# 48 float32r test matmuls behind the last product of a two-block decoder kernel

## The chip, the cores and the metric

The kernel runs on one core of a Trainium2 chip. The metric is device time in microseconds (us); the time before is the median of three runs. TensorE is called PE here, its weight loads PEld, VectorE DVE, ScalarE ACT, GpSimd POOL, and SyncE SP.

## The reference

Two transformer blocks on 256 tokens of width 1024. The part that matters here is the end of the second block, the last thing computed:

```python
h2 = rms_norm(x, norm_ffn_pre[l])
up = causal_depthwise_conv(h2 @ w_up[l], conv_w[l], conv_b[l])
g, v = jnp.split(up, 2, axis=-1)
ff = (jax.nn.gelu(g, approximate=True) * v) @ w_down[l]
x = x + rms_norm(ff, norm_ffn_post[l])
```

The rows of x are the result. All that stands before (two attention forms, a gated recurrence, cross attentions, pooling, a first feed-forward) is untouched by the change.

## The kernel before, in words

Every float32 product with a weight is carried by three float32r products: both operands are split into hi and lo, and hi*hi + hi*lo + lo*hi is accumulated in PSUM (`mm3`, lines 204 to 207). Each of these is one matmul of 128 stationary columns and 256 or 512 moving columns, with its own weight load.

The work is listed as a program of units and short pieces (`place`, `run`, `do`) and emitted in that order by `emit` (line 180). PE's instructions stand in just this order; the other engines take theirs as they are released. The last entries of the program come from `ffn` (line 558), called for the second block's feed-forward: eleven granules of 256 features, of which the last two are held back (`hold=2`). `close(t)` (line 594) issues their down products for token half t, column half by column half, through `down` (line 569) and `mm3`. These write the PSUM tiles named `s`; the moving operand is a weight row of 512 contiguous float32r values. `second` (line 505) closes token half 1, and its last product, L207, is the last instruction of PE before the end of the program.

Behind it stands the end of the computation, in `Last` (line 482) and the helpers that it inherits: ACT squares the column half and sums it (L303), DVE adds the two sums (L309), POOL raises the result to the power -1/2 (L296), DVE multiplies the row by the gain (L434) and adds it to the residual in three column quarters (L474), ACT and POOL do the fourth one (L492, L493), and SP stores each quarter with a DMA (L494). Then the program ends (L1397): every engine waits until its own work is done (DRAIN), SP waits for the stores, and a barrier joins the engines.

PSUM has three groups of tiles: `mm` and `tp` with two buffers each, `s` with four. The `tp` tiles (`tp_t`, line 85) hold transposes and small products; the last use of one in the program is a transpose of the gate columns early in this feed-forward. `xh` and `xl` are the hi and lo parts of the normed, transposed input of the feed-forward, 128 partitions by 8 by 256 values each; `eh` is such a tile for the memory rows.

Of the kernel before, what the change touches and what calls it, by code (L numbers as in the profile page):

```python
# [18 lines left out]
P = 128  # L19
T = 256  # L20
# [10 lines left out]
class Granule:  # L31
    """2048 weights per partition: one load, split in two parts as they are needed."""
# [7 lines left out]
def two_blocks(ctx: ExitStack, tc: tile.TileContext, a: dict, out: bass.AP):  # L40
    """Every float32 product with a weight is carried by three float32r passes:
    both operands are split exactly as hi + lo with hi = float32r(v), lo = v - hi,
    and hi*hi + hi*lo + lo*hi is accumulated in PSUM.

    Stationary/moving forms:
      a_units: weight blocks stationary, x^T moving  -> [feature, token]
      b_units: x^T blocks stationary, weights moving -> [token, feature]

    The work is first listed as a program of units (one weight part each, with short
    pieces attached), then emitted in that order; loads and splits run ahead of it.  # L50
    """
# [19 lines left out]
    # ------------------------------------------------------------------ tiles  # L71
# [38 lines left out]
    # ------------------------------------------------------------------ program and weight stream  # L110
    stream = []
# [53 lines left out]
    def place(fn, gran=None, pieces=()):  # L165
        """Append one unit; gran: the granule that it is the first to use."""
        if gran is not None:
            stream.append(gran)
        prog.append((fn, list(pieces)))

    def run(units, at=None):
        """List the units in order; at[i] are short pieces that follow unit i."""
        at = at or {}
        for i, (fn, gran) in enumerate(units):
            place(fn, gran, at.get(i, ()))
# [4 lines left out]
    def emit():  # L180
        """Per unit: its products, what earlier units left to do, the next split, its own results, its pieces."""
        for fn, pieces in prog:
            evac = fn() if fn is not None else None
            todo = later[:]
            later.clear()
            for f in todo:
                f()
            if fn is not None:
                pump()
            if evac is not None:  # L190
                evac()
            for f in pieces:
                f()

    def then(*fns):
        """Emit the first function in the next unit, the second one in the unit after that, and so on."""
        def go():
            fns[0]()
            if fns[1:]:
                then(*fns[1:])  # L200
        later.append(go)

    # ------------------------------------------------------------------ products
# [5 lines left out]
    def a_units(src, xt, evac, nk=8):  # L209
        """One granule [nk*128, c] (nk*c = 2048) in two units: evac(i, psum[128, 512]) per pair of blocks."""  # L210
# [25 lines left out]
    def b_part(w, xt, t, k0, o, first, last):  # L236
        """o[128 tokens of half t, 512] += x[:, k0*128...] @ w, w = (hi, lo) [128, 2, 512]."""
        tok = slice(t * P, (t + 1) * P)
        for k in range(2):
            mm3(o, r32(xt[0][:, k0 + k, tok]), r32(xt[1][:, k0 + k, tok]), w[0][:, k, :], w[1][:, k, :],  # L240
                first and k == 0, last and k == 1)

    def b_units(src, xt, evac):
        """[token, 512] = x @ w[:, 512 columns] in four units of two k blocks; evac(t, psum[128, 512])."""
# [29 lines left out]
    def grid(w, c0, n, dst, scale=None, xt=XT):  # L274
        """n granules of feature-major output written to dst[128, n*512]."""
        u = []
        for g in range(n):
            u += a_units(cols(w, c0, g), xt, ev_to(dst[:, g * 512:(g + 1) * 512], scale))
        return u

    def rows(w, c0, n, dst, xt=XT):
        """n times 512 columns of token-major output written to dst[128, 2, n*512]."""
# [6 lines left out]
    # ------------------------------------------------------------------ norms  # L289
# [3 lines left out]
    def power(v, n):  # L293
        """v ** -0.5 on [128, n]."""
# [4 lines left out]
    def square(src, acc, eng=S):  # L299
        """acc = sum(src**2) / 1024 over one half row, [128, 512]."""  # L300
# [19 lines left out]
    def split_to(dst, sl, src, scale=None):  # L320
        """dst hi/lo [:, sl] from src; an optional per-partition scale."""
# [8 lines left out]
    def turn_rows(xn, t, dst, tile=tp_t):  # L330
        """[128 tokens of half t, 1024] -> x^T hi/lo."""
# [8 lines left out]
    # ------------------------------------------------------------------ attention pieces  # L340
    def turn_causal(pm):
        """pm [128 t, (tile0: 128 s | tile1: 256 s)] -> PSUM [s0: 256 t | s1: 128 t]."""
# [5 lines left out]
    def causal_exp(s, bias):  # L348
        """s: two PSUM tiles, tile0 in 0:128, tile1 in 128:384; bias [128, 256] is added to tile1 and, its
        second half, to tile0. Returns exp(s + bias - max) [128, 2, 384] and the sums [128, 4] in the order  # L350
        (side, tile)."""
# [14 lines left out]
    def full_softmax(s):  # L366
        """s: PSUM [128, 2, 256] -> normalised probabilities [128, 2, 256]."""
# [13 lines left out]
    def turn_full(pm):  # L381
        """[128 t, t-tile, 256 m] -> SBUF [128 m, m-tile, 256 t]."""
# [8 lines left out]
    class Heads:  # L391
        """Pieces per head: S(i) scores and exponentials, T(i) transposes, V(i) products with v."""
# [19 lines left out]
    # ------------------------------------------------------------------ residual stages  # L412
    class Tail:
        """What follows a residual product for one token half. o: its two column halves in PSUM.
        half(n) as half n is complete, finish() after both, turn() sends x^T to XT."""
# [16 lines left out]
        def times(self, src, n, i):  # L432
            """x = src * gain; the row's factor follows when it is known."""
# [6 lines left out]
        def renorm(self):  # L440
            """x = rmsnorm(h) * g1."""
# [14 lines left out]
    class BlockEnd(Tail):  # L456
        """h = rmsnorm(h + o) * g0 starts the second block; x = rmsnorm(h) * g1."""
# [5 lines left out]
    class PostNorm(Tail):  # L463
        """h += rmsnorm(o) * g0; then x = rmsnorm(h) * g1."""
# [17 lines left out]
    class Last(PostNorm):  # L482
        """out = h + rmsnorm(o) * g0."""
# [12 lines left out]
    def end_stage(tails, close, fill, lead=None):  # L496
        """close(t) ends the products of token half t. Behind it: fill, units without a part in this, or
        lead(t, ..), the first products of the next stage for one half, or nothing."""
# [18 lines left out]
    def out_stage(src, xt, tail, gains, fill=(), at=None, lead=None):  # L517
        """[token, 1024] = x @ src in column halves."""
# [39 lines left out]
    def ffn(ng, up, w_down, tail, gains, fill=(), hold=2, ahead=2):  # L558
        """up(i) -> (units, y): the up products of granule i and its y hi/lo [128, 2, 256]."""
# [47 lines left out]
    # ================================================================== start  # L607
# [23 lines left out]
    def start():  # L631
# [10 lines left out]
        # the tensor engine reaches its full clock only in steady work  # L642
# [30 lines left out]
        # vectors that are needed feature-major: rows of 128 values, turned by the tensor engine  # L673
# [21 lines left out]
        def vectors():  # L695
# [4 lines left out]
            # lower bound of the forget gate, [128, 4] for the four heads  # L700
# [10 lines left out]
        def tables():  # L711
# [4 lines left out]
            # row selectors: column h of sel has ones in rows h and 32 + h  # L716
# [18 lines left out]
        def difference():  # L735
            # lambda of the differential attention, the same on every partition
# [15 lines left out]
    # ================================================================== block 1  # L752
# [8 lines left out]
    # --- gated recurrence inputs, feature-major  # L761
# [20 lines left out]
    # --- the recurrence as a tree over block sizes: sibling blocks of size b meet with  # L782
    # q decayed from its block's start, k decayed to its block's end
# [11 lines left out]
    def later_blocks(b):  # L795
        """s[:, 64 * (4 * c + j):] = k^T q for the second of each two sibling blocks of 128 tokens."""
# [62 lines left out]
    def h_out(c):  # L859
        """o = attn^T gi for token half c, head norm and output gate; the transposes follow later."""  # L860
# [34 lines left out]
    # --- forgetting attention  # L895
    def forget():
        """-cumsum(log sigmoid(ff + bias)) as hi rows 0:8 and lo rows 32:40 of nF."""
# [66 lines left out]
    # --- memory rows for the cross attentions: normalised in place, turned later  # L964
# [28 lines left out]
    # --- the mixer  # L993
# [22 lines left out]
    # --- cross attention  # L1016
# [18 lines left out]
    # memory of the second block: keys and values are the fill of the coming norms  # L1035
# [15 lines left out]
    # --- feed-forward 1  # L1051
    def y_tiles(i):
        """two float32 scratch tiles and the hi/lo tiles of granule i, [128, 2, 256] each."""
# [19 lines left out]
    # ================================================================== block 2  # L1073
# [33 lines left out]
    # windowed means by doubling; the first w-1 tokens divide by their own count  # L1107
# [55 lines left out]
    # --- differential attention  # L1163
# [43 lines left out]
    def d_norm(q4):  # L1207
        """head norm of four heads, both token halves."""
# [53 lines left out]
    # --- feed-forward 2  # L1262
# [7 lines left out]
    def lead(t, turn):  # L1270
        """Gate columns 0:512 and the first k half of 512:1024, token-major: half t is ready before the other one."""
# [32 lines left out]
    def conv(o, y, j0):  # L1304
        """y[128, 2, 256] = causal depthwise convolution of two blocks along the tokens."""
# [43 lines left out]

    ffn(11, up2, a["w_down_2"][0], Last, lambda: [gain("norm_ffn_post_2")])  # L1350
    emit()


# [47 lines left out]
```

## Time and profile before

| | us |
|---|---|
| median of 3 runs | 923.94 |
| lowest, highest run | 923.03, 926.76 |
| span of the profiled execution (first to last instruction) | 918.8 |
| PE busy in it | 904.6 |
| median of the runs less that span | 5.1 |

The profiled execution has no time of its own beside its span; what lies around a span is taken as the last line of the table. PE busy is the union of its matmuls' times, and their ends are modelled, so the cost of one in a stream is read from the distance of the starts, not from its length.

### The profile page before, as it was taken

The numbers are of one execution on the slowest core, as the hardware profiler recorded it, in microseconds if no ns is written. First come the engines' busy times: TensorE is split into PE (matmuls) and PEld (weight loads), VectorE is DVE, ScalarE is ACT, GpSimd is POOL, SyncE is SP. The second block draws the span as 40 slices with busy tenths as digits, with TensorE's granted clock in tenths as the row PEclk, the third lists the DMA queues.
The fourth block names the chain that finished last, engine by engine and source line by source line (L and its number), as shares of the span: only waits on it lengthen the run. The fifth ranks groups of instructions, "written<-read, shape, count | busy, mean of one in ns | idle before, by whom it ended". The sixth has DMA issues, their size and how long they took to land.

```text
span 918.8 us, 15164 instructions
## 1 busy us (share of the span) xinstructions
PE 904.6 (98%) x6203; PEld 823.5 (90%) x6203; DVE 589.3 (64%) x861; ACT 489.4 (53%) x741; POOL 125.5 (14%) x134
## 2 busy tenths in 40 slices
PE   8999999999999999999999999999999999999996
PEld 7889799899899999999899899999998789999995
DVE  5787666764675554445686555776656777766664
ACT  6763644555455444444564454657443676555552
POOL 3200110000002111111104000221301201101101
PEclk9999999999999999999999999999999999999998
DMA  8774344544465555565374555334655455555531
GB/s 260 253 245 141 130 153 169 197 148 138 161 204 184 185 184 183 184 186 188 134 271 139 184 181 187 128 115 140 216 178 190 159 185 182 186 199 192 167 131 46
DMA packets 116819, 160.79 MB, mean 175 GB/s; under 512 B 4551, under 2 KB 89357, under 8 KB 116749
## 3 DMA queue, kind: packets, MB, share of 16 engines
q1 hardware_dynamic: 116749, 159.82, 52.2%
q8 instruction: 48, 0.79, 0.3%
q14 instruction: 22, 0.18, 0.1%
HBM read 158.76 MB, written 1.05 MB: 174 GB/s over the span
## 4 chain that ended last, share of the span: by engine, by line
PE 89%; DVE 3%; DMA 2%; ACT 2%; issue 1%; POOL 1%; SPq 1%; DVEq 0%; POOLq 0%; ACTq 0%
PE mm L205 19%; PE mm L206 19%; PE mm L207 19%; PE s L206 8%; PE s L207 8%; PE s L205 8%; DMA w<-in_w_in_dram 2%; DVE wl L142 1%; PE s L804 1%; PE tp L336 1%; POOL sm L296 1%; PE tp L1032 1%; PE s L1024 1%; ACT wh L141 1%; DMA lamv<-in_lambda_k_dram 1%
## 5 line engine op out<-in xcount | busy, mean ns | idle before, releaser
L142 DVE TENSOR_TENSOR wl<-w,wh 128x1024 fp32r<-128x1024 f32 x283 | 354.0, 1257 | 191.8 <-ACT wh L141 190.1
L141 ACT CAST wh<-w 128x1024 fp32r<-128x1024 f32 x284 | 296.8, 1051 | 305.6 <-PE mm L206 199.2
L205 PE MATMUL mm<-xh,wh 128*128 128x256 f32 x1120 | 317.5, 283 | 0.4 <-ACT r L765 0.4
L206 PE MATMUL mm<-xl,wh 128*128 128x256 f32 x1120 | 313.1, 280 | 0.3
L207 PE MATMUL mm<-xh,wl 128*128 128x256 f32 x1120 | 312.5, 279 | 0.0
L205 PEld LDWEIGHTS mm<-xh,wh 128*128 128x128 f32 x1120 | 210.6, 188 | 4.3 <-issue 2.0
L206 PEld LDWEIGHTS mm<-xl,wh 128*128 128x128 f32 x1120 | 210.6, 188 | 2.1 <-DVE xl L328 0.7
L207 PEld LDWEIGHTS mm<-xh,wl 128*128 128x128 f32 x1120 | 210.5, 188 | 0.0
L205 PE MATMUL s<-wh,mh 128*128 128x512 f32 x176 | 70.1, 398 | 0.0
L206 PE MATMUL s<-wl,mh 128*128 128x512 f32 x176 | 69.6, 395 | 0.0
L207 PE MATMUL s<-wh,ml 128*128 128x512 f32 x168 | 66.4, 395 | 0.0
L296 POOL TENSOR_TENSOR sm<-sm,half 128x1 f32<-128x1 f32 (+2 forms) x24 | 20.2, 842 | 214.9 <-DVE sm L309 203.9
L1067 POOL TENSOR_TENSOR r<-r 128x512 f32<-128x512 f32 x16 | 25.4, 1584 | 149.1 <-ACT r L1065 149.1
L205 PE MATMUL mm<-eh,wh 128*128 128x256 f32 x160 | 45.6, 285 | 0.0
L206 PE MATMUL mm<-el,wh 128*128 128x256 f32 x160 | 44.7, 279 | 0.0
L207 PE MATMUL mm<-eh,wl 128*128 128x256 f32 x160 | 44.6, 279 | 0.0
L207 PE MATMUL s<-wh,mh 128*128 128x512 f32 x112 | 44.3, 396 | 0.0
L1326 POOL TENSOR_TENSOR r<-r 128x512 f32<-128x512 f32 x11 | 21.4, 1946 | 148.6 <-DVE r L1314 124.8
L206 PE MATMUL s<-wl,ml 128*128 128x512 f32 x104 | 41.1, 396 | 0.0
L205 PE MATMUL s<-wh,ml 128*128 128x512 f32 x104 | 41.1, 395 | 0.0
L205 PE MATMUL mm<-wh,xh 128*128 128x512 f32 x96 | 39.4, 410 | 0.5 <-ACT xh L324 0.4
L206 PEld LDWEIGHTS s<-wl,mh 128*128 128x128 f32 x176 | 33.1, 188 | 7.2
(272 smaller groups left out, 1365.3 us busy)
## 6 DMA issues: line engine op xcount, KB each, us to landing
w<-in_w_in_dram SPq DMA_DIRECT2D x41, 1024.0 KB, 5.3
w<-in_w_dram SPq DMA_DIRECT2D x32, 1024.0 KB, 4.8
w<-in_w_up_dram SPq DMA_DIRECT2D x22, 1024.0 KB, 5.0
w<-in_w_down_dram SPq DMA_DIRECT2D x11, 1024.0 KB, 5.1
w<-in_w_xkv_dram SPq DMA_DIRECT2D x8, 1024.0 KB
w<-in_w_out_dram SPq DMA_DIRECT2D x8, 1024.0 KB, 6.1
w<-in_w_xq_dram SPq DMA_DIRECT2D x4, 1024.0 KB, 4.7
w<-in_w_xo_dram SPq DMA_DIRECT2D x4, 1024.0 KB, 5.8
```

The costliest lines, as they stand in the source:

```text
L141: S.copy(hi, src)
L142: low.tensor_tensor(lo, src, hi.bitcast(F32), op=ALU.subtract)
L205: PE.matmul(o, lh, rh, start=first, stop=False)
L206: PE.matmul(o, lh, rl, start=False, stop=False)
L207: PE.matmul(o, ll, rh, start=False, stop=last)
L296: G.tensor_tensor(r[:, :n], v[:, :n], half.to_broadcast([P, n]), op=ALU.pow)
L336: PE.transpose(o[:, k * P:(k + 1) * P], xn[:, kk * P:(kk + 1) * P], ident)
L804: PE.matmul(o, k_[:, x], q2, start=True, stop=True)
L1024: PE.matmul(s[:, t, :], xq[:, j, t * P:(t + 1) * P], xkT[:, j, :], start=(c == 0), stop=(c == 1))
L1032: PE.matmul(o[:, c * T:(c + 1) * T], xv[:, m, cs], pt[:, m, :], start=(m == 0), stop=(m == 1))
L1067: G.tensor_tensor(tt, ra, ra, op=ALU.mult)
L1326: G.tensor_tensor(yv, yg, yv, op=ALU.mult)
```

## The change

At the end of the program, ahead of `emit()`, a piece `after` is added (`do(after)`). It takes two `tp` tiles and issues twelve groups of four matmuls into them in turn. All multiply float32r values of `xh` as moving columns by 128 stationary columns of `xl` (in one group `eh`), and nothing reads their results. Nine of the groups move 512 columns of the first 512 or so values of a row or of values 1024 to 1535; six of those visit them out of order. `runs(x, b, f)` cuts a row into b blocks, and takes f columns of the first block, f of the second one and so on, then the next f of each. Group by group: contiguous; the same with stationary columns of `eh`; runs of 4 from 2 blocks; of 2 from 2; of 16 from 2; of 4 from 64; of 4 from 32; of 4 from 8; contiguous at 1024; contiguous from column 2; 256 columns only; four runs of 128, 512 apart. That is 44 matmuls of 512 columns and 4 of 256. The change also takes the comments and docstrings out, which moves no line ahead of `after`.

```diff
     ffn(11, up2, a["w_down_2"][0], Last, lambda: [gain("norm_ffn_post_2")])
+
+    def after():
+        flat = r32(xh.rearrange("p k t -> p (k t)"))
+        near = flat[:, 0:512]
+        lhs, lhs_e = r32(xl[:, 0, 0:P]), r32(eh[:, 0, 0:P])
+        o1, o2 = tp_t(), tp_t()
+
+        def runs(x, b, f):
+            return x.rearrange("p (b n f) -> p n b f", b=b, f=f)
+
+        def four(o, lh, rh):
+            n = 1
+            for m in rh.shape[1:]:
+                n *= m
+            o = o[:, 0:n]
+            if len(rh.shape) == 4:
+                o = o.rearrange("p (a b c) -> p a b c", b=rh.shape[2], c=rh.shape[3])
+            for i in range(4):
+                PE.matmul(o, lh, rh, start=(i == 0), stop=(i == 3))
+
+        for i, (lh, rh) in enumerate((
+                (lhs, near),
+                (lhs_e, near),
+                (lhs, runs(near, 2, 4)),
+                (lhs, runs(near, 2, 2)),
+                (lhs, runs(near, 2, 16)),
+                (lhs, runs(near, 64, 4)),
+                (lhs, runs(near, 32, 4)),
+                (lhs, runs(near, 8, 4)),
+                (lhs, flat[:, 1024:1536]),
+                (lhs, flat[:, 2:514]),
+                (lhs, flat[:, 0:256]),
+                (lhs, flat[:, 0:2048].rearrange("p (b f) -> p b f", b=4)[:, :, 0:128]),
+        )):
+            four((o1, o2)[i % 2], lh, rh)
+    do(after)
     emit()
```

The end of PE's instructions, before (-) and with the change (+); `s_7537` is the PSUM tile of the last column half, `tp_9044` and `tp_9045` are the two tiles of `after`, and "x4" stands for four in a row:

```order
 L206 MATMUL s_7537<-wl_8964,ml 128x512
 L207 MATMUL s_7537<-wh_8963,ml 128x512
-L1397 UNCONDITIONAL_BRANCH
+L1372 MATMUL tp_9044<-xh,xl 128x512 [waits PE_49]
+L1372 MATMUL tp_9044<-xh,xl 128x512 x3
+L1372 MATMUL tp_9045<-xh,eh 128x512 [waits PE_49]
+L1372 MATMUL tp_9045<-xh,eh 128x512 x3
```

Behind these follow the other ten groups in the same way, and then the branch that ends PE's program; the two new waits are on PE's own earlier work, and no matmul of before has moved.

The end of SP's instructions, which is the same in both kernels but for the line number of the branch:

```order
178 L494 DMA out_dram<-h 128x256 [waits DVE_49]
179 L494 DMA out_dram<-h 128x256 [waits DMAHW6_49,DVE_49]
180 L494 DMA out_dram<-h 128x256 [waits DMAHW7_49,DVE_49]
181 L494 DMA out_dram<-h 128x256 [waits DMAHW0_49,Pool_49]
182 L1397 UNCONDITIONAL_BRANCH
```

The stores wait for DVE, for POOL and for queue places; none of them waits for PE.

## Rows read from the trace of the kernel before

**Rows 1.** The page: busy us (share of the span) and instructions, one engine a line.
```profile
PE 904.6 (98%) x6203; PEld 823.5 (90%) x6203; DVE 589.3 (64%) x861; ACT 489.4 (53%) x741; POOL 125.5 (14%) x134
```
**Rows 2.** Stretches at the end: length, busy us of each engine, granted clock, DMA share, GB/s.
```profile
900.00:911.60 11.60, 11.60 (x51) 9.19 (x49) 4.64 (x8) 3.19 (x8) 1.94 (x3) 1.00 0.14 45
911.60:914.00 2.40, 0.21 (x1) 0.00 (x0) 1.31 (x4) 1.16 (x3) 0.55 (x1) 1.00 0.00 0
914.00:918.70 4.70, 0.00 (x0) 0.00 (x0) 1.25 (x2) 0.04 (x1) 0.85 (x1) 0.50 0.34 113
```
**Rows 3.** Timeline of the end: start us, length us, engine, line, op, count, [idle before].
```profile
910.71 0.40 PE L207 MATMUL s<-wh,ml 128*128 128x512 f32 x1
...
911.41 0.40 PE L207 MATMUL s<-wh,ml 128*128 128x512 f32 x1
911.90 0.60 ACT L303 ACTIVATE junk<-s 128x512 bf16<-128x512 f32 x1 [2.11 <-PE s L207]
...
912.92 0.55 POOL L296 TENSOR_TENSOR sm<-sm,half 128x1 f32<-128x1 f32 x1 [3.59 <-DVE sm L309]
913.50 1.75 DVE L474 SCALAR_TENSOR_TENSOR h<-r,sm,h 128x256 f32<-128x256 f32 x3
```
**Rows 4.** The stores L494 and the ending L1397: count, duration ns min/median/max, first and last start.
```profile
L494 SPq DMA_DIRECT2D out_dram<-h x8: 332/359/430, 908.4 to 915.7; - x8
...
L1397 SPq DRAIN  x3: 7/7/7, 918.0 to 918.3; - x3
...
L1397 PEldq DRAIN  x2: 13/2200/4388, 907.5 to 918.4; - x2
```
**Rows 5.** Waits of SP from 900 us on: who for whom, total us, times, longest.
```profile
SPq L1397 <- DMA out_dram<-h: 1.2, 1, 1.2
```
**Rows 6.** Timeline of PE: a stream of 256-column float32r products, first and last shown.
```profile
128.08 0.28 PE L206 MATMUL mm<-el,wh 128*128 128x256 f32 x1
...
129.95 0.28 PE L207 MATMUL mm<-eh,wl 128*128 128x256 f32 x1
```
**Rows 7.** Timeline of PE: contiguous float32 products of the cross attention, 256 columns.
```profile
197.12 1.89 PE L1024 MATMUL s<-r,r 128*128 128x256 f32 x8
```
**Rows 8.** Timeline of PE: float32 products with broken moving columns, one row a level.
```profile
60.25 1.89 PE L804 MATMUL s<-r,r 128*128 128x64 f32 x16
64.84 1.89 PE L804 MATMUL s<-r,r 128*128 128x64 f32 x16
...
78.60 1.89 PE L804 MATMUL s<-r,r 128*128 128x64 f32 x16
```

## The prediction

> **What bounds the kernel now.** I read the page first, then the end of the timeline, then the ending itself. PE is busy for 904.6 of 918.8 us [rows 1], so it sets the time up to its last product. What matters here comes after that: the change adds nothing ahead of it. The last product starts at 911.41 [rows 3], and in the 4.70 us from 914.00 on PE does nothing at all [rows 2]. In this tail ACT takes up the last column half at 911.90, POOL's power follows at 912.92 and DVE's sums with the residual from 913.50 [rows 3]; the last store is issued at 915.7 [rows 4], SP waits 1.2 us for it to land [rows 5], and SP's first DRAIN of the ending is at 918.0 [rows 4]. The span ends 0.8 us later, at 918.8. So the tail is a chain of ACT, DVE, POOL, SP and a DMA, with PE waiting in the barrier.
>
> **The change, part by part.** Nothing is removed or moved. 48 matmuls, each with its weight load, go behind the last product on PE; nobody reads what they write. The results of the tail don't hang on them: ACT's squares wait for the product that stood there before. No SP, POOL or DMA instruction is added. So the tests run under the tail, from where the next product would have started, and only what sticks out behind it costs time.
>
> *One contiguous test of 512 columns.* The last products of 512 float32r columns start at 910.71 and, three steps on, at 911.41 [rows 3]: 0.2333 us a step, at a granted clock of 1.00 [rows 2], which is the level of 2.4 GHz. The modelled length of 0.40 us is latency, and is paid once, by the last one.
>
> *One test of 256 columns.* From 128.08 to 129.95 there are 16 steps [rows 6]: 0.117 us each. It is just half of the other, so the step goes by columns, and the weight load beside it adds nothing.
>
> *The two waits on PE's own work* are for the earlier writers of the `tp` tiles, transposes of long before. I take 0 for them; were they to hold until the last product is complete, the cost would be its length less one step, 0.40 - 0.23 = 0.2 us [rows 3], once.
>
> *The orders.* Six groups, 24 matmuls, visit their columns in runs of 2, 4 or 16; the other contiguous pieces I cost as contiguous. The trace of before has no float32r matmul with broken columns, so I bound it. From below: the float32 products of 256 contiguous columns are recorded as 8 pieces in 1.89 us, of which the last is some 0.38 long, so (1.89 - 0.38) / 7 = 0.216 us a piece [rows 7]. If I take such a piece to pass 512 columns through the array, which is 0.213 us at 2.4 GHz, then float32r loses 0.02 us a matmul to something that float32 doesn't have, and I take it to be the reading of its columns; an order that reads better could win that 0.02 back, in all 44 tests 0.8 us. From above: the float32 products of L804 read 64 columns in runs of 1, 2, 4 and on to 32 with gaps as long, one level a row. From the level with runs of 2 on, every level takes 1.89 us for 16 pieces [rows 8], or (1.89 - 0.27) / 15 = 0.108 us a piece, whatever the run. Runs of 2 or 4 thus cost no more than 0.108 us for 64 columns, eight times which is 0.86 us for 512: at most 0.63 us over the contiguous step, 15 us for the 24. That is a weak bound, since these pieces are alike because something else (most likely the weight load) sets their pace. The same rows say that the length of the run has never been seen to matter, so I take the contiguous step for all orders.
>
> *The sum.* 44 x 0.2333 + 4 x 0.117 = 10.7 us of steps. The first test starts one step behind 911.41, at 911.64; the last one starts at 911.64 + 10.7 - 0.23 = 922.14 and ends 0.40 later, at 922.54. PE's long DRAIN of before lasts from 907.5 for 4.388 us, to 911.89 [rows 4], or 0.08 us beyond the end of the last product. So PE is through at 922.62, where SP was at 918.0. The ending behind it takes the same 0.8 us (0.75 by the unrounded rows) and the span ends at 923.4, **4.6 us** later than before. The span of 918.8 stands 5.1 us below the median of the runs, and I leave that as it is: 923.94 + 4.6 = **928.5 us**. 0.5%, about what a measurement of this kernel can tell from no change, is 4.6 us, so the likeliest case lies just on that line.
>
> **The rivals.**
>
> *Only the finest order costs.* If float32r's reading fetches a few neighbouring columns at a time, and the 0.02 us by which it lags the columns' rate [rows 3, 7] shows that this fetch sets its pace, then runs of 2 use half of each fetch and their four matmuls take two steps each: 4 x 0.2333 = 0.9 us more, 929.4. Against it: the levels of runs of 2 and of 4 go at one pace in [rows 8]. The Trainium skill ("SBUF — State Buffer", Specifications (TRN2)) says that SBUF is read in lines of 16 bytes, that two hits a line are needed for full bandwidth and that each crossing to a new line pays a penalty. By that rule runs of 4 and 16 cost what contiguous columns do, and runs of 2, which make twice the crossings, are the one order that could cost more. No row here shows a broken float32r order.
>
> *Broken orders cost up to a second pass.* If a jump costs a read of its own, the 24 broken matmuls take between 0.05 and 0.23 us more each, 1.2 to 5.6 us together: 929.8 to 934.2. For it: float32r already runs 0.02 us behind the columns' own rate [rows 3, 7], so its reading has no room to spare. Against it: runs of 2 and of 32 are alike in [rows 8], though at a pace that would hide a doubling.
>
> *They cost more than that*, up to the bound of 0.63 us each: 934.2 to 943.7. Nothing in the trace excludes it; nothing hints at it.
>
> *The clock falls.* From 914.00 on the granted clock is 0.50 [rows 2], the level of 1.2 GHz, after PE had idled for some 2 us. Should it fall while the tests run, they would take twice their 10.7 us and the time would be about 939. Against it: in the stretch to 911.60 PE streams such matmuls at a clock of 1.00, and the tests go on without a gap.
>
> *The tests stay under the tail: not slower.* The mechanism: PE joins the barrier no later than SP does. For this the last test must have ended at 918.0 - 0.08, and started at 917.5: 47 steps in 5.9 us, 0.125 us each. Above that point each 0.01 us a step costs 0.5 us; below it the time stays at 923.9. For it: some 6 us of PE's time in the tail are free. Against it: 0.2333 us in the rows of the same shape just ahead, with the clock at its upper level [rows 2, 3]. The Trainium skill ("TensorE: Matmul & The Clock Gate", Back-to-back issue gap) gives about 131 ns for a matmul of 512 columns in a sustained stream with weight loads; by that figure PE would be through at about 918 and almost nothing would stick out. The trace disagrees, with 233 ns, and I follow the trace.
>
> **How the numbers follow.** Chances: all orders as contiguous 0.42, by itself 927.5 to 929.6 (0.8 us that better orders could win, 0.2 us for the first wait, and 0.9 us, the distance of the lowest run from the median); only the finest order 0.13; up to a second pass 0.26; more than that 0.12; the clock 0.04; under the tail 0.03. The range from 927.4 to 934.5 takes in the first three and leaves out the others, 0.19. Slower by over 0.5%: somewhat less than half of the first, 0.17, as it lies on the line, and 0.13 + 0.26 + 0.12 + 0.04, together 0.72. Within 0.5%: the other 0.25 of the first and 0.02 of the last, 0.27. Faster: 0.01, a run of the last that came out low.
>
> **What would show it.** The tests on line 1372 should start at 911.6, at 0.233 us a step for the contiguous groups and 0.117 for the short one, with a clock of 1.00 until they end at about 922.5. The step within each group of four tells the price of its order at once. SP should reach its DRAIN near 918.0 as before, and then wait for PE; the chain of waits should end on PE instead of on SP's store. The prediction is wrong if SP's DRAIN stays the last to arrive, if a group steps at over 0.3 us, if the clock falls before the last group, or if the tail itself (ACT at 911.9, the last store at 915.7) is later than before.

## The result and the profile after

The changed kernel takes 928.32 us (median of 18 runs, 926.55 to 930.90) against 923.14 us before (18 runs). The ratio is 1.0056, 95% interval 1.0044 to 1.0067: 5.2 us (4.1 to 6.2) slower, inside the range and on the side that was forecast. The 928.5 us of the prediction owes some of its closeness to luck: it added 4.6 us to a median of three runs, 923.94; the change costs 0.6 us more, and the median of 18 runs is 0.8 us lower. The two misses cancel.

The page of the changed kernel, its span and the busy time of the engines; they answer to [rows 1]:

```profile
span 924.9 us, 15260 instructions
## 1 busy us (share of the span) xinstructions
PE 916.1 (99%) x6251; PEld 832.5 (90%) x6251; DVE 590.3 (64%) x861; ACT 489.2 (53%) x741; POOL 124.2 (13%) x134
```

48 more records on PE and on PEld, none anywhere else. The span is 6.1 us longer than that of before. 0.87 us of it is older than the tests: the last product starts at 912.28 here and at 911.41 in [rows 3]. What is left is 5.2 us, as in the times. (Wherever a run's time and span are both on record they lie 1.7 to 1.9 us apart, so 3.3 of the 5.1 us that the table of before puts around its span come from a profiled execution quicker than the median; the prediction's sum, which adds to the median, is not touched.) The timeline of the end, with the columns of [rows 3]:

```profile
912.28 0.40 PE L207 MATMUL s<-wh,ml 128*128 128x512 f32 x1
912.52 1.09 PE L1372 MATMUL tp<-xh,xl 128*128 128x512 f32 x4
912.77 0.60 ACT L303 ACTIVATE junk<-s 128x512 bf16<-128x512 f32 x1 [2.11 <-PE s L207]
...
913.44 1.07 PE L1372 MATMUL tp<-xh,eh 128*128 128x512 f32 x4
...
913.79 0.55 POOL L296 TENSOR_TENSOR sm<-sm,half 128x1 f32<-128x1 f32 x1 [3.60 <-DVE sm L309]
914.35 9.70 PE L1372 MATMUL tp<-xh,xl 128*128 128x512 f32 x40
914.37 1.75 DVE L474 SCALAR_TENSOR_TENSOR h<-r,sm,h 128x256 f32<-128x256 f32 x3
```

The tests begin one step behind the last product. The tail beside them is as it was: ACT starts 0.49 us behind the start of the last product, as before, and POOL 1.51 us behind it, as before. The tests' end is 914.35 + 9.70 = 924.05. The stretches of the end, with the columns of [rows 2]:

```profile
911.60:914.00 2.40, 2.40 (x12) 1.96 (x11) 0.51 (x2) 0.69 (x2) 0.21 (x1) 1.00 0.42 140
914.00:922.00 8.00, 8.00 (x33) 5.97 (x32) 2.06 (x4) 0.51 (x1) 1.19 (x2) 1.00 0.20 67
922.00:924.90 2.90, 2.05 (x11) 1.42 (x9) 0.00 (x0) 0.00 (x0) 0.00 (x0) 1.00 0.00 0
```

PE is busy throughout and the granted clock stays at 1.00, where it had been 0.50 from 914.00 on. The ending, as in [rows 4], and SP's waits, as in [rows 5]:

```profile
L494 SPq DMA_DIRECT2D out_dram<-h x8: 332/369/1268, 909.2 to 916.6; - x8
...
L1436 SPq DRAIN  x3: 7/7/7, 924.1 to 924.4; - x3
...
L1436 PEldq DRAIN  x2: 13/2010/4007, 920.1 to 924.5; - x2
```

```profile
SPq L1436 <- PE tp L1372: 5.3, 1, 5.3
SPq L1436 <- DMA out_dram<-h: 1.2, 1, 1.2
```

The last store is issued 4.3 us behind the start of the last product, as before. The 5.3 us that SP now waits for the tests is the cost: SP's first DRAIN comes at 924.1 instead of 918.0, and 0.8 us later the span ends, as before.

The distance from each test to the next start gives each order's price. Ten groups, not nine as the description of the change has it, move 512 columns out of one stretch: four contiguous, six broken. From the starts in the trace, mean of a group's four steps (three for the last group) in ns:

```
contiguous, xl / eh / at 1024 / from column 2    232 / 228 / 229 / 236
256 columns; four runs of 128, 512 apart         119; 233
runs of 4, neighbours 32 / 64 / 256 / 1024 bytes apart   231 / 231 / 274 / 252
runs of 2, 1024 apart; runs of 16, 1024 apart    337; 243
```

Against 233 a step, the broken groups of runs of 2, of 4 (at 256 and 1024 bytes) and of 16 cost 0.42, 0.16, 0.07 and 0.04 us; the rest balances to within 0.05 us. That is the 0.6 us between 4.6 and 5.2.

### The profile page after: what moved, and what is told of

Read it like the earlier page. It is cut to its first block, busy times and chain, and to the rows that moved or that the text cites. A ratio compares the mean times of both kernels' runs of the same rounds, so it can differ in the third digit from the quotient of the medians.

```text
span 924.9 us, 15260 instructions
## 1 busy us (share of the span) xinstructions
PE 916.1 (99%) x6251; PEld 832.5 (90%) x6251; DVE 590.3 (64%) x861; ACT 489.2 (53%) x741; POOL 124.2 (13%) x134
## 3 DMA queue, kind: packets, MB, share of 16 engines
HBM read 158.76 MB, written 1.05 MB: 173 GB/s over the span
## 4 chain that ended last, share of the span: by engine, by line
PE 90%; DVE 3%; DMA 2%; ACT 2%; issue 1%; SPq 1%; POOL 1%; POOLq 0%; DVEq 0%; ACTq 0%
PE mm L205 19%; PE mm L206 19%; PE mm L207 19%; PE s L206 8%; PE s L207 8%; PE s L205 8%; DMA w<-in_w_in_dram 2%; DVE wl L142 1%; PE tp L1372 1%; PE s L804 1%; PE tp L336 1%; PE s L1024 1%; PE tp L1032 1%; POOL sm L296 1%; DMA lamv<-in_lambda_k_dram 1%
```

## The experiments

### Does the price belong to the order or to what runs beside it?

```diff
         for i, (lh, rh) in enumerate((
+                (lhs, flat[:, 0:2048].rearrange("p (b f) -> p b f", b=4)[:, :, 0:128]),
+                (lhs, flat[:, 0:256]),
...
+                (lhs_e, near),
                 (lhs, near),
-                (lhs_e, near),
-                (lhs, runs(near, 2, 4)),
...
```

> The same twelve groups of four, last one first. In the changed kernel the groups of runs of 4, 2 and 16 from 2 blocks (0.252, 0.337 and 0.243 us a step) ran in the first 5 us behind the last product, beside the residual's end and the stores; runs of 4 from 8 blocks (0.274) ran later, alone. Theory, the price belongs to the order: each group keeps its step within 0.01 us wherever it stands, and PE's tests take 11.4 us together again. Rival, the price is the company: the three groups fall to 0.233 us when they stand last, some contiguous ones rise in their place, and runs of 4 from 8 blocks, now in the fifth place, change too.

Measured: 327 ns for the runs of 2, 277 for the runs of 4 from 8 blocks, 251 and 239 for runs of 4 and 16 from 2 blocks, 226 and 232 for runs of 4 from 32 and 64, contiguous groups 231 to 233; from the first start to the last one 11.09 us against 11.14. Every group kept its step within 0.010 us, wherever it stood. The price belongs to the order and not to what runs beside it.

### Does the tail cover half of the tests?

Three kernels replace the table by one kind of test: 24 or 48 contiguous ones, or 48 in runs of 2 from 2 blocks. The first has six lines `(lhs, near)` in the table, the second twelve:

```diff
                 (lhs, near),
-                (lhs_e, near),
-                (lhs, runs(near, 2, 4)),
...
+                (lhs, near),
+                (lhs, near),
...
```

and the third has twelve lines with runs of 2:

```diff
-                (lhs, near),
-                (lhs_e, near),
-                (lhs, runs(near, 2, 4)),
                 (lhs, runs(near, 2, 2)),
...
+                (lhs, runs(near, 2, 2)),
+                (lhs, runs(near, 2, 2)),
...
```

> 24 contiguous tests of 512 columns instead of the 48. Theory, only what sticks out behind the last store costs time: 24 x 0.233 = 5.6 us of steps, PE is through some 5.9 us behind the start of its last product's follower, while the stores are awaited until 6.4 us behind it, so the time is that of before within 0.5 us. Rival, work behind the last product costs its whole length: 5.6 us over before, 0.6%.

> 48 contiguous tests of 512 columns. Theory: 48 x 0.233 = 11.2 us of steps, about 5.1 us over the kernel before (ratio 1.0055). The difference to the changed kernel is then what its orders cost (0.6 us) less what its short group saves (0.5 us), near nothing. Rival, full length: 11.2 us over.

> 48 tests, all in runs of 2 from 2 blocks. Theory, the price belongs to the order: 0.337 us at every step, 16.2 us of steps, PE through at 10.1 us behind the stores, so 10.1 us over the kernel before and 5.0 us over the one with 48 contiguous tests. Rival, the price is the company of the tail: 0.337 us only for the first 16 or so, then 0.233, 6.7 us over before.

Measured against the kernel before on the same chip (922.25 us): 24 tests ratio 1.0004 (0.9991 to 1.0018), 48 contiguous 1.0046 (1.0032 to 1.0060), or 4.2 us, 48 in runs of 2 1.0097 (1.0081 to 1.0113), or 9.0 us. SP's waits of the ending, with 24 tests:

```profile
SPq L1430 <- DMA out_dram<-h: 1.3, 1, 1.3
SPq L1430 <- PEq L1430: 0.6, 2, 0.4
```

and with 48 in runs of 2:

```profile
SPq L1436 <- PE tp L1372: 9.7, 1, 9.7
SPq L1436 <- DMA out_dram<-h: 1.3, 1, 1.3
```

With 24 there is no wait for a test: they end under the stores. With the dear ones the wait is 9.7 us, with 48 contiguous ones 4.9 us, and both times agree with their wait within their intervals. The rival that each test costs its length is out. Both waits lie a little below the expected 10.1 and 5.1 us because repeated tests step faster than assumed: 227 ns instead of 233 contiguous, 328 instead of 337 in runs of 2. The dear steps go on to the last test, long after the tail, so the rival that the price is the company of the tail falls here as well.

### The same tests without the cover

```diff
-    ffn(11, up2, a["w_down_2"][0], Last, lambda: [gain("norm_ffn_post_2")])
 
     def after():
...
     do(after)
+    ffn(11, up2, a["w_down_2"][0], Last, lambda: [gain("norm_ffn_post_2")])
     emit()
```

> The same 48 tests, issued ahead of the second feed-forward's up products instead of behind the last product, where PE never waits long. Theory, the tail is what covers half of them: here nothing does, and the time is 11.4 us over the kernel before, less at most 1 or 2 us where PE would have waited for weights right behind; 6 us more than the changed kernel. Rival, PE has slack enough to absorb them anywhere: about 5 us over, as behind the last product.

Measured: ratio 1.0116 (1.0094 to 1.0138), 10.7 us over before (921.24 us), twice the price of the same work behind the last product. The groups step as they do there (runs of 2 at 337 ns). At this place PE has no slack that would absorb them; other places were not tried.

### What sets the price of an order?

24 orders of the same 512 columns, 8 matmuls each, behind the last product:

```diff
+            for i in range(8):
...
                 (lhs, runs(near, 64, 4)),
                 (lhs, runs(near, 32, 4)),
+                (lhs, runs(near, 16, 4)),
...
+                (lhs, runs(near, 2, 16)),
```

> 24 groups of 8 matmuls behind the last product, each group one order of the same 512 columns: runs of f columns taken in turn from b blocks, so neighbouring runs lie 2048/b bytes apart. So far runs of 4 cost nothing at distances of 32 and 64 bytes, 0.277 us a step at 256 bytes, 0.25 at 1024; runs of 2 cost 0.33 at 1024. Distance theory: a step depends on how far one run lies from the next; then runs of 2 and of 1 at 64 bytes or less also go at 0.23 us, and runs of 4, 8 and 16 at 256 bytes are all dearer than at 1024. Filling theory: a fetch brings some 4 columns and what is not taken from it is lost; then runs of 2 take 0.33 us or more and runs of 1 over 0.45 us at every distance, also at 16 and 32 bytes, and runs of 8 and 16 are never over 0.25 us. Turn theory: each end of a run costs a fixed time, whatever the distance; already hard to hold with the free runs of 4, it would put runs of 1 at 0.43 us and runs of 2 at 0.33 at every distance and runs of 8 between 0.23 and 0.24.

Mean of the seven steps within a group in ns, by the length of the runs and the distance between the starts of neighbouring runs:

```
bytes apart      8    16    32    64   128   256   512  1024
runs of 1      450   460     -   434     -   494     -   219
runs of 2        -   449   463   433   447   501   444   330
runs of 4        -     -   233   224   246   275   269   252
runs of 8        -     -     -   233     -   248     -   244
runs of 16       -     -     -     -   238   239     -   240
```

The filling theory comes nearest: runs of 2 and 1 are dear even at 16 and 8 bytes, so distance alone is not the cause, and runs of 8 and 16 stay under 250. It misses at runs of 1 that are 64 bytes apart (434, not over 450), and it has no reason for the 224 to 275 of runs of 4. The turn theory falls: up to 256 bytes runs of 2 cost about what runs of 1 do (433 to 501 against 434 to 494), and not 330. But none of the three explains the last entry of the first line. Single columns in turn from two halves are **faster than contiguous**: 215 to 216 ns after the first, 512 columns at one a cycle of 2.4 GHz and 2 ns.

### What holds a contiguous float32r matmul back?

```diff
+                [(lhs, near), (lhs_e, near)],
+                [(lhs, near), (lhs_e, far)],
...
+                [(lhs[:, 0:64], near)],
+                [(lhs[:, 0:32], near)],
...
+                [(zb[:, 0:P], zb)],
```

The last line shown is the bfloat16 group; `zb` holds zeros.

> 15 groups of 8 contiguous matmuls behind the last product; the products of the kernel step at 0.233 us, a test that is repeated with the same operands at 0.227, and 512 columns at one a cycle of 2.4 GHz would be 0.213. Theory, float32r's reading of moving columns is what is slower: 64 or 32 stationary columns change nothing, bfloat16 goes at 0.213 to 0.216 us, and the moving operand's alternating between places brings 0.227 to 0.233. Rival, the weight load beside it takes part of the reading: 32 stationary columns bring float32r to 0.22 us or less, and 256 moving columns with 64 stationary ones go below 0.113. A third possibility: changing the stationary operand from one matmul to the next is what costs the 0.006 us; then the group that alternates between two of them stands at 0.233 and the one that alternates the moving operand at 0.227.

Measured, 8 matmuls a group: repeated operands 227 ns, and so are alternating stationary, alternating moving, and both. With 64 and 32 stationary columns 231 and 233, not less. bfloat16 216, and a piece of a float32 product also 216. For 512 columns the weight load and the change of operands are out as causes. With 256 moving columns that is less clear: 64 stationary columns brought the step from 118 to 114 ns, which is just short of the rival's mark (below 113) but more than the theory's nothing, and it stays unexplained. What is left as the cause is the moving read of float32r; the next experiment tests it, with the same data in another order. Why the kernel's products stand at 233 and repeated tests at 227 isn't explained by any of these groups and stays open.

### Two columns of different lines in turn

```diff
+        def turns(x, f):
+            return x.rearrange("p (n b f) -> p n f b", b=2, f=f)
...
+        def pairs(x):
+            return x.rearrange("p (b n) -> p n b", b=2)
...
+                [(lhs, pairs(near))],
+                [(lhs, turns(near, 4))],
+                [(lhs, turns(near, 2))],
```

> 13 groups of 8 matmuls behind the last product. The survey of orders held one that was faster than contiguous: single columns in turn from two halves, 1024 bytes apart, 0.2157 us a step, while single columns from 8 or more places cost 0.43 to 0.49. Stream theory: PE takes visited columns two at a time, and the first and the second of each pair fetch 16-byte lines on their own; the step goes by how many columns such a stream takes from a line in a row: 4 gives 0.216, 2 (contiguous columns) 0.227 to 0.233, 1 gives 0.33 to 0.5. Then all orders with two columns of different lines in turn are fast, at any distance: turns of 4 (columns 0,4,1,5,2,6,3,7 and so on, 16 bytes apart), of 8 and of 32, and the wide one (4096 bytes apart) at 0.216; turns of 2 (0,2,1,3) at 0.227 to 0.233 as contiguous ones; single columns from four quarters, where each stream changes its line at every step, at 0.43 to 0.49; 256 columns in turn at 0.107 to 0.110 against 0.117. Distance theory: only places of 1024 bytes or more apart are fast; turns of 4, 8 and 32 cost 0.25 to 0.5. Two-place theory: any order that goes between two places is fast, turns of 2 as well (0.216).

Measured in ns: pairs 216; turns of 4, 8 and 32 columns 216, 216, 216; 4096 bytes apart 216; turns of 2 232; contiguous 230; four quarters 281; 256 columns in turn 111 to 112 against 122. The stream theory named the fast and the slow ones, and both rivals fall on turns of 4 (16 bytes apart, fast) and turns of 2 (two places, not fast). It misses at the four quarters, dearer than contiguous but not 430, and slightly at the 256 columns, for which it had 107 to 110.

The Trainium skill ("SBUF — State Buffer", Specifications (TRN2)) says that SBUF has lines of 16 bytes which need two hits or more for full bandwidth. The runs agree with lines of that size, but not with two hits being enough: contiguous columns, which hit each line four times in a row, are slower (230 ns) than turns of 4, which change the line at every column (216), and the measurement decides. What fits for float32r is to count the hits for every second visited column apart: a contiguous order then has two a line and falls short by 5 to 8%, and four a line reach the full rate. It leaves open why runs of 4, which have two a line as well, take from 224 to 275. That PE reads in two such streams fits the steps; nothing here shows it directly.

### A faster kernel from it

Only moving weights are turned, stationary operands and the order in PSUM stay as they are: the splits store hi and lo of the 512-column weights in the order that the turns undo. `mm3_turns` stands in the place of `mm3` in `b_part` and `down`; the kernel with the store order alone leaves out the first two lines of its body, so that its columns come out in another order. There are no tests in these kernels.

```diff
+        if not g.by_col:
...
+            src = flat(src).rearrange("p (q n b) -> p q b n", b=2, n=256)
+            hi, lo = (flat(x).rearrange("p (q b n) -> p q b n", b=2, n=256) for x in (hi, lo))
...
+    def mm3_turns(o, lh, ll, rh, rl, first, last):
+        o = o.rearrange("p (n b) -> p n b", b=2)
+        rh, rl = (x.rearrange("p (b n) -> p n b", b=2) for x in (rh, rl))
+        mm3(o, lh, ll, rh, rl, first, last)
```

> The kernel before, without any test, but all float32r products of 512 moving weight columns visit them in turn from two halves: their hi and lo parts are stored in that order (each split reads its source at every second column), so the results come out in place. Stream theory: about 1416 such products save 0.2333 - 0.2157 = 0.0176 us each, 25 us, and the time is 898 us (ratio 0.973) if the splits on ACT and DVE keep their pace. Rival: reading the source at every second column doubles the splits' reading on ACT (1.05 us now) and DVE (1.25 us now); they are needed about every 2.8 us of PE's time, so PE begins to wait for weights and half or more of the gain is lost: 910 us or more. Second rival: the fast step belongs to a stream of tests that repeat their operands and not to products; then nothing changes, 923 us.

> The same store order of the weight columns, but the products visit them as they lie; the columns of all such products come out in another order. It takes the faster visiting away and leaves what the stores cost. Stream theory: within 2 us of the kernel before if the splits keep their pace; if the splits suffer, slower than before by what they cost, and the difference to the kernel with both parts is the gain of the visiting alone, about 25 us.

Measured: 906.35 us, ratio 0.9836 (0.9819 to 0.9853) to the kernel before (922.17 us): 15 us faster, between the 25 of the theory and the 12 or less of the first rival. With the store order alone 1.0002 (0.9991 to 1.0012). So the gain is the visiting. Timeline of the kernel with turned weights:

```profile
880.11 1.59 ACT L146 CAST wh<-w 128x1024 fp32r<-128x1024 f32 x1 [0.67 <-PE mm L211]
880.25 0.38 PE L211 MATMUL s<-wl,mh 128*128 128x512 f32 x1
...
881.33 0.38 PE L210 MATMUL s<-wh,mh 128*128 128x512 f32 x1
...
881.73 1.50 DVE L147 TENSOR_TENSOR wl<-w,wh 128x1024 fp32r<-128x1024 f32 x1 [1.88 <-ACT wh L146]
```

The same splits in the kernel before:

```profile
894.93 1.05 ACT L141 CAST wh<-w 128x1024 fp32r<-128x1024 f32 x1 [0.74 <-PE mm L206]
...
896.01 1.23 DVE L142 TENSOR_TENSOR wl<-w,wh 128x1024 fp32r<-128x1024 f32 x1 [1.42 <-ACT wh L141]
```

The products step at 0.216 us ((881.33 - 880.25) / 5), as forecast, and by the distances of starts 1366 of 1415 did. But the split beside them takes 1.59 us on ACT instead of 1.05, and 1.50 on DVE instead of 1.23; 48 of ACT's 284 splits are over 1.4 us, the others under 1.3, most near 1.05. Over the whole trace the starts that came late (over 260 ns behind a 512-column product, the rest of a step counted) grew from 7.0 to 14.6 us, which is some 8 of the missing 10 us. Of these 8 us, 1.4 are products at half the clock, and most of the others are waits of PE that are new or have grown: for DVE (norms, an elementwise product) and for ACT (hi parts of activations). None of PE's waits ends on a weight split, so what the longer splits cost PE can only come by way of the queues of ACT and DVE, and how much it is isn't shown. The stretch at half the clock stands behind such a wait. Timeline and stretch of the kernel with turned weights:

```profile
450.44 0.38 PE L212 MATMUL mm<-wh,el 128*128 128x512 f32 x1
452.43 0.63 PE L346 MATMUL tp<-ident,r 128*128 128x128 f32 x4 [1.61 <-DVE r L448]
```

```profile
453.36:456.77 3.41, 3.41 (x10) 2.91 (x11) 3.41 (x5) 0.91 (x2) 0.00 (x0) 0.50 0.74 258
```

Here the granted clock was 0.50, the level of 1.2 GHz, and the products stepped at 0.427 us; before and after it was 1.00. The next kernel keeps the turns and changes their distance:

```diff
-            src = flat(src).rearrange("p (q n b) -> p q b n", b=2, n=256)
...
+            src = flat(src).rearrange("p (q f b) -> p q b f", b=2, f=8)
...
-        rh, rl = (x.rearrange("p (b n) -> p n b", b=2) for x in (rh, rl))
+        rh, rl = (x.rearrange("p (n b f) -> p n f b", b=2, f=8) for x in (rh, rl))
```

> As the kernel with turned weights, but in turns of 8: columns 0,8,1,9 and so on within each 16, 32 bytes apart instead of 1024, and stored so by the splits. There 48 of the 284 ACT splits took 1.5 to 1.7 us instead of 1.05 to 1.13, with PE streaming turned products beside them, and PE's waits behind products grew by 9 us. Theory, the distance of 1024 bytes collides with ACT's reading: the splits go back to 1.05 to 1.15 us and the time falls by some us, to 900 to 904. Rival, what the splits meet is PE's reading at full rate together with their own reading of every second column: they stay at 1.5 us or more and the time at 906 within 2 us. Second rival, shorter runs make the splits themselves dearer: over 909 us.

Measured: 903.3 us, ratio 0.9793 (0.9772 to 0.9814), apart from that of the kernel above: 19 us under before (921.88 us). The splits on ACT (count, ns min/median/max), first with 1024 bytes between the two places, then with 32:

```profile
L146 ACT CAST wh<-w x284: 1029/1054/1702, 14.7 to 880.1; 128x1024 fp32r<-128x1024 f32 x142
```

```profile
L146 ACT CAST wh<-w x284: 1027/1054/1193, 15.9 to 881.2; 128x1024 fp32r<-128x1024 f32 x142
```

As the first theory had it, the distance decides: no split over 1.2 us is left. With the store order of 1024 bytes but PE reading contiguously the longest was 1.17 us, so the split's own order does not do it; it takes PE's turned reading beside it. The split's order changed together with PE's distance, and no run parts the two. The profiled span, 904.1 us, is no shorter than the other's 903.8, and the clock has a part in that. The same stretch, first in the kernel with 1024 bytes, then with 32:

```profile
52.60:59.40 6.80, 6.80 (x60) 6.10 (x60) 5.78 (x8) 4.91 (x10) 0.55 (x1) 1.00 0.91 320
```

```profile
52.60:59.40 6.80, 6.80 (x34) 6.80 (x33) 3.67 (x5) 1.34 (x4) 0.52 (x1) 0.50 0.84 330
```

With 32 bytes PE had just waited 2.38 us for DVE, the granted clock was 0.50 here, and 34 matmuls were issued instead of 60. Of the 0.4% between the two kernels a part may be the clock's as well: with a mean granted clock of 0.992 or 0.993 they took 905.9 us (32 bytes) and 906.4 to 907.6 (1024). What is shown clean are the splits. PE's late starts still sum to 11.2 us, the next thing to work on.

## Why the prediction was right, point by point

- **The tests run under the tail and cost what sticks out.** Right: SP waits 5.3 us for them, 24 of them cost nothing that can be measured, and without the cover all 48 cost 10.7 us.
- **The contiguous step, 0.2333 us.** Right to within 3%: 0.228 to 0.236 in the changed kernel, 0.227 for tests that only repeat.
- **"I take the contiguous step for all orders."** Wrong in its letter, by 0.6 us of 11.1 (first start to last). Four of the six broken groups cost something, runs of 2 most: 0.42 us for four matmuls. The rival of the finest order had 0.9 us for them, that of a second pass 1.2 to 5.6 us for all; the truth lies between the likeliest case and the first of these, and is neither: runs of 4 at 256 bytes, free by that rival, took 0.274 us. The measured time stands inside the likeliest case's own 927.5 to 929.6 all the same, which is the luck of the two medians. (The lower end of these doesn't follow from its terms: 928.5 - 0.8 - 0.9 is 926.8.) One of the prediction's signs of being wrong came true: a group stepped at over 0.3 us, the runs of 2 at 0.337. The bound from the float32 rows was as weak as it was called: their 0.108 us a piece hid that runs of 1 and 2 halve float32r's pace at most distances.
- **The two waits on PE's own work.** Right: the first test starts 0.235 us behind the last product, one step.
- **The clock.** Right: 1.00 to the end.
- **The ending.** The 0.08 and 0.8 us hold. One sign was put wrongly: SP's DRAIN doesn't come at 918.0 and wait afterwards. SP waits for PE first and drains then, at 924.1.
- **"An order that reads better could win that 0.02 back."** The prediction named it for the lower end of its range alone. It is true of an order that the change did not hold: single columns in turn win 0.018 us (0.2157 against the 0.2333 of the products).
- **The 131 ns of the Trainium skill** ("TensorE: Matmul & The Clock Gate", Back-to-back issue gap) for 512 columns in a stream: no run here comes near it; the fastest step of 512 columns, bfloat16 included, is 215.7 ns.

## What to carry to other kernels

Work put behind the last product of a PE-bound kernel is free up to the point where the output's own chain ends, here about 25 matmuls (an estimate from the 6 us between the first test and the stores' landing; 24 were free, 48 were not), and costs its full step from there on; the ending's waits of SP show which of the two came last. That makes the tail a good place to measure an operation by itself, and the prices found there held in the middle of the program.

Where float32r products bound a kernel, let the moving operand visit two places in turn, four columns apart or more (two were not enough), and store it so that the results come out in place: that took 2.1% off this kernel. Afterwards look at the engines that feed PE, which have less time for the same work.

## What was not expected of the hardware

- Contiguous float32r columns aren't the fastest order: 227 to 233 ns for 512, against 216 in turns of two places, 16 to 4096 bytes apart; 216 is also what bfloat16 (zeros) takes.
- Pairs taken from four places or more and single columns from eight or more cost 433 to 501 ns, twice the contiguous step, but pairs from two halves 330 and single columns from four quarters 281; runs of 4 at 256 bytes cost more (275) than at 32, 64 or 1024 (233, 224, 252). The cause of these differences is open.
- PE's turned reading at a distance of 1024 bytes lengthened ACT's split of every second column from 1.05 to 1.59 us; at 32 bytes, with the split's order changed to match, it did not.
